# Weight tiles written three ahead of their products, pair sums in pieces and 512 KB loads in a split-precision decoder layer

## The chip, the cores and the metric

The program runs on one core of one Trainium2 chip, as a single launch. The metric is the device time of an execution in microseconds; a kernel's time is the median of its runs. The engines are named as the profile names them: PE (matrix products), PEld (its weight loads), DVE (vector), ACT (scalar), POOL, and SP, which here does nothing but issue DMAs.

## The reference

One decoder layer on 256 tokens of width 4096. All matrices are float32.

```
proj = x @ w_in                          # 4096 x 11280
y_conv = conv_group(c_a, c_b) * silu(c_gate)
y_gla  = gla_group(g_q, g_k, g_v, g_lr) * silu(g_gate)
y_mem  = memory_group(m_q, mem @ w_mem_kv) * silu(m_gate)   # 256 memory tokens, 4096 x 2048
out = concat(y_conv, y_gla, y_mem) @ w_out                  # 4096 x 4096
y = layernorm(ALPHA * x + out, ln_g, ln_b)
```

## The kernel before, in words

Every large product is done in split precision. A weight tile arrives in SBUF as float32 (`raw`); ACT casts it to `hi` (line 89), DVE subtracts `hi` from `raw` to get `lo` (line 90; both in the helper `halves`), and PE does three products for each tile of the activations, which are split in the same way: hi with hi, hi with lo, lo with hi. PE so can't start on a weight tile before ACT has cast it, and can't end it before DVE has made the rest.

The work has four stages in this order.

- **Memory stage** (lines 150 to 192). 32 steps `kt` over the rows of `w_mem`; each step takes 128 rows of 2048 columns, 1024 KB. The first 1024 columns (`mk`) and the last 1024 (`mv`) are two halves of one `raw` tile, split and multiplied apart. After the first step a step's 1024 KB come with one DMA (line 162). Every fourth step a 512 KB unit of the memory tokens (`rawmem`) and one of the tokens x (`rawx`, for the later stages) are loaded and split.
- **Panels** (`panel`, line 277). 23 column panels of `w_in`, each in 8 loads of 1024 KB and 16 weight tiles. The elementwise work of convolution, attention and gates waits in a list, and is taken off it (`do_work`) behind the tiles.
- **Pairs** (`pair`, line 353). Three pairs of 512 output columns of `w_out`, 16 chunks each. A chunk is done either with eight block products or with seven, by Winograd's form of Strassen's method; in the second case DVE makes combinations `tx` and `ty` of the four weight blocks first (lines 398 to 411), and the activations' combinations `eh`, `el` come from `make_sums` (`sums`, line 332, with scratch tiles `r` and `f`). Eight PSUM banks hold a pair's partial products (`N`, `4`, `3`, `2`, `1`, `5`, `6`, `7`). Behind a pair the banks are added into four tiles of the residual `z`, statistics are taken and a row of `ln_g` is multiplied in (lines 1085 to 1115): 20 DVE instructions. The scratch `U` of these sums, `tx` and `f` share one buffer (tag `T`), `ty` and `r` another (tag `S`).
- **Last two panels and the layer norm** (lines 1119 to 1152).

All pools rotate: three `raw` buffers, four `hi` and four `lo`. The text of the kernel does not set the order on an engine: the program is built with `tile.TileContext(nc, schedule_with_timeline_sim=True)` (line 1232), and a scheduler places the instructions of each engine by a timeline of its own, with the text's order as the wish. On the chip each engine then works its list strictly from the top. All loads are issued by SP; eight completion semaphores rotate, and in the built program a load waits until the one eight places ahead of it in SP's list has landed.

Of the kernel before, what the change touches and what calls it, by code (L numbers as in the profile page):

```python
# [9 lines left out]
F32 = mybir.dt.float32  # L10
# [18 lines left out]
EARLY = 5  # L29

# [18 lines left out]
def layer_kernel(ctx, tc, xT, memT, xres, w_mem, w_in, w_pairs, w_last, cst, w_gate,  # L49
# [103 lines left out]
    for kt in range(KT):  # L153
# [123 lines left out]
    def panel(chunks, width, stat, fills=0, apart=0, soon=KT // 2):  # L277
# [3 lines left out]
        for tt in range(2):  # L281
            serial[0] += 1
            banks.append(acc.tile([P, 512], F32, tag="acc", name=f"acc_{serial[0]}"))
        held = []
# [14 lines left out]
        for c in range(KT // 2):  # L299
            if c % 2 == 0:  # L300
                raw = w_raw([P, 4, width], "w")
                nc.sync.dma_start(out=raw, in_=chunks[c // 2].rearrange("p (k n) -> p k n", k=4))
            hi, lo = w_tiles([P, 2, width], "w", KT // 2 - apart <= c < KT // 2 - WBUFS)
            halves(raw[:, 2 * (c % 2) : 2 * (c % 2) + 2, :], hi, lo)
            if c >= KT // 2 - apart:
                held.append((c, hi, lo))
            else:
                for w in (hi, lo):
                    for tt in range(2):
                        mms(c, tt, w, w is lo)  # L310
            left = max(1, soon - c)
            do_work(-(-len(work) // left))
            for _ in range(min(fills, len(fill))):
                fill.popleft()()
        if not apart:
            return banks

        def rest(k, tt):
            c, hi, lo = held[k]
            for w in (hi, lo):  # L320
                mms(c, tt, w, w is lo)

        return banks, rest
# [29 lines left out]
    def pair(chunks, order, stat, ext, soon=KT // 2):  # L353
# [3 lines left out]
        for pool, tag, names in ((acc, "acc", "N432"), (sm, "sm", "1567")):  # L357
            for nm in names:
                serial[0] += 1
                banks[nm] = pool.tile([P, 512], F32, tag=tag, name=f"{tag}_{nm}_{serial[0]}")  # L360

# [28 lines left out]
        for n, (c, by7, tiles) in enumerate(plan):  # L390
            raw = w_raw([P, 4, 512], "w")
            nc.sync.dma_start(out=raw, in_=chunks[c].rearrange("p (k n) -> p k n", k=4))
            w = {}
            if by7:
                serial[0] += 1
                x = tmp.tile([P, 2, 512], F32, tag="T", name=f"tx_{serial[0]}", bufs=1)
                y = tmp.tile([P, 2, 512], F32, tag="S", name=f"ty_{serial[0]}", bufs=1)
                nc.vector.tensor_tensor(
                    out=x,
                    in0=raw[:, 3:4, :].to_broadcast([P, 2, 512]),  # L400
                    in1=raw[:, 0:3:2, :],
                    op=ALU.subtract,
                )
                nc.vector.tensor_tensor(
                    out=y[:, 0, :], in0=raw[:, 2, :], in1=x[:, 0, :], op=ALU.subtract
                )
                nc.vector.tensor_tensor(
                    out=y[:, 1, :], in0=raw[:, 1, :], in1=y[:, 0, :], op=ALU.subtract
                )
                src = dict(a=raw[:, 0:2, :], c=raw[:, 2:3, :], x=x, y=y)  # L410
            else:
                src = dict(a=raw[:, 0:2, :], b=raw[:, 2:4, :])
            for nm, terms in tiles:
                m = 1 if nm == "c" else 2
                w[nm] = tuple(t[:, :m, :] for t in w_tiles([P, 2, 512], "w"))
                halves(src[nm], *w[nm])
                for second in range(2):
                    for j, (slot, st, bk) in enumerate(terms):
                        sh, sl = st(c)
                        for s in (sh,) if second else (sh, sl):  # L420
                            nc.tensor.matmul(  # L421
                                banks[bk],
                                lhsT=s,
                                rhs=w[nm][second][:, slot, :],
                                start=first[bk] == (n, nm, j) and not second and s is sh,
                                stop=last[bk] == (n, nm, j) and second == 1,
                            )
            do_work(-(-len(work) // max(1, soon - n)))
        return banks
# [405 lines left out]
    off = 0  # L835
    for name, i, ranges in PANELS:
        width = sum(n for _, n in ranges)
        size = 16 * P * 2 * width
        chunks = w_in[off : off + size].rearrange("(c p f) -> c p f", c=8, p=P)
        off += size  # L840
        banks = panel(chunks, width, lambda u: x_units[u], fills=2)
# [87 lines left out]
    for hi, lo in x_units:  # L929
        give(hi, lo)  # L930
    assert not fill
# [144 lines left out]
    for u in (4, 5):  # L1076
        work.append(lambda u=u: make_sums(u))
    for j in range(3):
        if j == 1:
            work.append(lambda: make_sums(6))  # L1080
        n0, n1 = 2 * j, 2 * j + 1
        load_res(n0)
        load_res(n1)
        b = pair(w_pairs[j], orders[j], stat, lambda u: extT[u], soon=KT // 2 if j else 8)
        rows = [spread(ln_g, n0, "Ah"), spread(ln_g, n1, "Al")]

        def add(y, ps, first=False):
            if first:
                nc.vector.scalar_tensor_tensor(
                    out=y, in0=y, scalar=ALPHA, in1=ps, op0=ALU.mult, op1=ALU.add  # L1090
                )
            else:
                nc.vector.tensor_tensor(out=y, in0=y, in1=ps, op=ALU.add)  # L1093

        z11, z21 = z[n0][:, 0, :], z[n0][:, 1, :]
        z12, z22 = z[n1][:, 0, :], z[n1][:, 1, :]
        add(z22, b["N"], True)
        add(z12, b["3"], True)
        add(z11, b["2"], True)
        add(z21, b["4"], True)  # L1100
        serial[0] += 1
        t = tmp.tile([P, 2, 512], F32, tag="T", name=f"U_{serial[0]}", bufs=1)
        u2, u3 = t[:, 0, :], t[:, 1, :]
        nc.scalar.copy(out=u2, in_=b["1"])
        add(z11, b["1"])
        nc.vector.tensor_tensor(out=u2, in0=u2, in1=b["6"], op=ALU.add)
        add(z12, b["5"])
        add(z22, b["5"])
        nc.vector.tensor_tensor(out=u3, in0=u2, in1=b["7"], op=ALU.add)
        add(z12, u2)  # L1110
        add(z21, u3)
        add(z22, u3)
        for n, tt, y in ((n0, 0, z11), (n1, 0, z12), (n0, 1, z21), (n1, 1, z22)):
            nc.vector.bn_stats(out=stats[:, tt, n, :], in_=y)
            nc.vector.tensor_tensor(out=y, in0=y, in1=rows[n - n0], op=ALU.mult)  # L1115
    for e in extT.values():
        give(*e)
# [126 lines left out]
```

## Time and profile before

| | us |
|---|---|
| median of 3 runs (1563.94 to 1565.36) | 1564.78 |
| the profiled execution | 1562.82 |
| its span, first to last instruction | 1561.1 |
| PE busy | 1523.4 |
| DVE busy | 1069.3 |
| ACT busy | 769.7 |

The span is what the trace shows; the profiled execution's own time has 1.7 us more that lie around it. Busy times of different engines overlap and don't add up.

### The profile page before, as it was taken

What the parts mean: (1) busy time and instruction counts of PE and PEld (TensorE: products, weight loads), DVE (VectorE), ACT (ScalarE), POOL (GpSimd) and SP (SyncE); (2) the same over time, 40 slices, a digit from 0 to 9 for tenths busy, and PEclk for the clock granted to TensorE, in tenths of its full rate; (3) what the DMA queues carried; (4) which work ended last, traced back from release to release, by engine and by line L of the source; (5) the groups of instructions that cost most, each with busy time, mean ns of one, the idle gap of its engine ahead of it and who ended that gap; (6) DMA issues with size and microseconds to landing.
All of it is one profiled execution on the core that took longest, in us unless ns stands there. A gap on an engine that the chain in (4) does not pass through costs nothing.

```text
span 1561.1 us, 18190 instructions
## 1 busy us (share of the span) xinstructions
PE 1523.4 (98%) x6929; PEld 1288.4 (83%) x6929; DVE 1069.3 (68%) x1361; ACT 769.7 (49%) x936; POOL 46.8 (3%) x59
## 2 busy tenths in 40 slices
PE   7999999999999999999999999999999998989997
PEld 5888888888888888999998888888888876878885
DVE  6554564999999555757574555556576697887965
ACT  6443454444465444664454554455555434545541
POOL 0000000000000000003030000000000000000001
PEclk9999999999999999999999999999999998999998
DMA  9665555555555655455545555555567545546562
GB/s 358 245 216 191 192 199 199 180 199 189 189 172 180 216 189 189 158 191 174 173 158 198 189 191 212 189 191 195 199 225 269 189 162 196 195 175 217 206 219 108
DMA packets 49184, 307.52 MB, mean 197 GB/s; under 512 B 5508, under 2 KB 6404, under 8 KB 18504
## 3 DMA queue, kind: packets, MB, share of 16 engines
q1 hardware_dynamic: 49096, 306.36, 55.8%
q8 instruction: 54, 0.88, 0.2%
q14 instruction: 34, 0.28, 0.0%
HBM read 302.14 MB, written 4.19 MB: 196 GB/s over the span
## 4 chain that ended last, share of the span: by engine, by line
PE 94%; DVE 3%; DMA 2%; issue 0%; ACT 0%; SPq 0%; POOL 0%; DVEq 0%; ACTq 0%
PE acc L291 67%; PE acc L421 9%; PE mk L181 5%; PE mv L181 5%; PE sm L421 3%; PE acc_N L421 3%; DMA rawwm<-w_mem 1%; DMA rawx<-xT 1%; DVE low L90 1%; PE o L272 1%; PE A L682 1%; DVE xr L1093 0%; PE sc L272 0%; PE mo L272 0%; DVE xr L1115 0%
## 5 line engine op out<-in xcount | busy, mean ns | idle before, releaser
L90 DVE TENSOR_TENSOR low<-raww,hiw 128x1024 fp32r<-128x1024 f32 (+3 forms) x496 | 586.3, 1187 | 329.5 <-ACT hiw L89 316.2
L89 ACT CAST hiw<-raww 128x1024 fp32r<-128x1024 f32 (+3 forms) x496 | 499.4, 1012 | 556.3 <-PE acc L291 470.6
L291 PE MATMUL acc<-hiw,hx 128*128 128x512 f32 (+2 forms) x1472 | 560.3, 381 | 0.0
L291 PE MATMUL acc<-hiw,lx 128*128 128x512 f32 (+2 forms) x1472 | 560.3, 381 | 0.0
L291 PE MATMUL acc<-low,hx 128*128 128x512 f32 (+2 forms) x1472 | 381.6, 380 | 0.0
L291 PEld LDWEIGHTS acc<-hiw,hx 128*128 128x128 f32 x1472 | 276.3, 188 | 45.4
L291 PEld LDWEIGHTS acc<-hiw,lx 128*128 128x128 f32 x1472 | 276.3, 188 | 45.2
L291 PEld LDWEIGHTS acc<-low,hx 128*128 128x128 f32 x1472 | 275.2, 188 | 45.5
L90 DVE TENSOR_TENSOR lowm<-rawwm,hiwm 128x1024 fp32r<-128x1024 f32 (+2 forms) x68 | 78.5, 1161 | 77.7 <-ACT hiwm L89 75.7
L89 ACT CAST hiwm<-rawwm 128x1024 fp32r<-128x1024 f32 (+2 forms) x68 | 67.7, 1003 | 89.4 <-PE mk L181 41.3
L421 PE MATMUL acc<-hiw,xh 128*128 128x512 f32 x224 | 88.0, 393 | 16.2 <-ACT hiw L89 16.2
L770 DVE SCALAR_TENSOR_TENSOR cacc<-hT,cst_sb,cacc 128x231 f32<-128x231 f32 (+29 forms) x240 | 97.9, 461 | 0.1
L421 PE MATMUL acc<-hiw,xl 128*128 128x512 f32 x224 | 87.6, 391 | 0.0
L421 PE MATMUL acc<-low,xh 128*128 128x512 f32 x224 | 66.9, 390 | 0.0
L421 PEld LDWEIGHTS acc<-hiw,xh 128*128 128x128 f32 x224 | 42.2, 189 | 25.8 <-ACT hiw L89 17.1
L181 PE MATMUL mk<-hiwm,hmem 128*128 128x512 f32 (+1 forms) x132 | 52.3, 398 | 9.3 <-ACT hiwm L89 9.3
L181 PE MATMUL mk<-hiwm,lmem 128*128 128x512 f32 (+1 forms) x132 | 51.8, 394 | 0.0
L239 ACT COPY S<-T 32x256 f32<-32x256 f32 x112 | 45.2, 404 | 9.9 <-DVE T L224 8.5
L181 PE MATMUL mv<-hiwm,hmem 128*128 128x512 f32 x128 | 50.0, 391 | 0.0
L291 PE MATMUL acc<-hiw,xh 128*128 128x512 f32 x128 | 49.9, 390 | 0.0
L181 PE MATMUL mv<-hiwm,lmem 128*128 128x512 f32 x128 | 49.8, 389 | 0.0
L291 PE MATMUL acc<-hiw,xl 128*128 128x512 f32 x128 | 49.8, 389 | 0.0
(231 smaller groups left out, 1327.9 us busy)
## 6 DMA issues: line engine op xcount, KB each, us to landing
raww<-w_in SPq DMA_DIRECT2D x144, 1024.0 KB
raww<-w_pairs SPq DMA_DIRECT2D x48, 1024.0 KB
rawwm<-w_mem SPq DMA_DIRECT2D x31, 1024.0 KB
raww<-w_in SPq DMA_DIRECT2D x32, 824.0 KB
raww<-w_last SPq DMA_DIRECT2D x16, 1024.0 KB
raww<-w_in SPq DMA_DIRECT2D x8, 832.0 KB
rawx<-xT SPq DMA_DIRECT2D x8, 512.0 KB
xr<-xres SPq DMA_DIRECT2D x8, 512.0 KB
```

Of the source, the lines that this page charges most:

```text
L89: nc.scalar.copy(out=hi, in_=src)
L90: nc.vector.tensor_tensor(out=lo, in0=src, in1=hi.bitcast(F32), op=ALU.subtract)
L181: nc.tensor.matmul(mem_banks[half * 4 + a // 512 * 2 + mt][:, a % 512 : a % 512 + step], lhsT=s[:, kt % 4, mt * P : (mt + 1) * P], rhs=w[: ...
L239: f(out=to[32 * b : 32 * b + 32, :, :, a, :], in_=frm[32 * a : 32 * a + 32, :, :, b, :],)
L272: nc.tensor.matmul(ps, lhsT=a, rhs=b, start=t == 0 and k == 0, stop=t == n - 1 and k == 2)
L291: nc.tensor.matmul(banks[tt][:, :width], lhsT=s[:, kt % 4, tt * P : (tt + 1) * P], rhs=w[:, k, :], start=kt == 0 and not second and s is s ...
L421: nc.tensor.matmul(banks[bk], lhsT=s, rhs=w[nm][second][:, slot, :], start=first[bk] == (n, nm, j) and not second and s is sh, stop=last[b ...
L682: nc.tensor.matmul(ps[:, at : at + n], lhsT=keys[:, j, k0 : k0 + P], rhs=qs[:, j, q0 : q0 + n], start=dk == 0, stop=dk == 1,)
L770: nc.vector.scalar_tensor_tensor(out=a, in0=h, scalar=dw_sb[:, cb, j : j + 1], in1=a, op0=ALU.mult, op1=ALU.add)
```

## The change

The halves of a memory step are loaded by a DMA of 512 KB each. Weight tiles pass through a queue, `stream`: `push` writes a tile's load and its split, and the products of a tile are written when three more tiles have been pushed (`AHEAD = 3`). What stands behind a pair or a panel (evacuations, sums, further loads) is hung on the last tile's products with `after`. A pair's sums fall into a first part (`close`) and pieces in a second queue, `later`, one of which is written behind each tile that follows. The pieces need one scratch tile `u2` in place of two, and 20 DVE instructions as before, in another order. PSUM banks of a pair are taken when first used.

```diff
         raw = w_raw([P, 2, 1024], "wm")
-        if kt:
-            nc.sync.dma_start(out=raw, in_=w_mem[kt].rearrange("p (h n) -> p h n", h=2))
         for half in range(2):
+            if kt:
+                nc.sync.dma_start(
+                    out=raw[:, half, :], in_=w_mem[kt][:, 1024 * half : 1024 * half + 1024]
+                )
             wt = (raw[:, half, :], *w_tiles([P, 1024], "wm"))
...
+    stream = deque()
+    later = deque()
+
+    def push(make, use):
+        make()
+        stream.append(use)
+        while len(stream) > AHEAD:
+            stream.popleft()()
+
+    def after(f):
+        if stream:
+            g = stream.pop()
+            stream.append(lambda: (g(), f()))
+        else:
+            f()
...
+        for c in range(KT // 2):
+            push(lambda c=c: make(c), lambda c=c: use(c))
+        after(lambda: then(banks))
...
+        for n, (_, _, tiles) in enumerate(plan):
+            for i in range(len(tiles)):
+                push(lambda n=n, i=i: make(n, i), lambda n=n, i=i: use(n, i))
+        after(lambda: then(banks))
...
+    def close(n0, b):
+        z11, z21 = z[n0][:, 0, :], z[n0][:, 1, :]
+        z12, z22 = z[n0 + 1][:, 0, :], z[n0 + 1][:, 1, :]
+        add(z22, b["N"], True)
+        add(z12, b["3"], True)
+        add(z21, b["4"], True)
+        add(z11, b["2"], True)
+        rows = [spread(ln_g, n0, "Ah"), spread(ln_g, n0 + 1, "Al")]
...
+        def one():
+            nc.scalar.copy(out=u2, in_=b["1"])
+            add(z11, b["1"])
+
+        def two():
+            add(u2, b["6"])
+            add(z12, b["5"])
+
+        def three():
+            add(z22, b["5"])
+            add(z12, u2)
+
+        def four():
+            add(u2, b["7"])
+            add(z21, u2)
+
+        def five():
+            add(z22, u2)
+
+        def stat_scale(n, tt):
+            y = z[n][:, tt, :]
+            nc.vector.bn_stats(out=stats[:, tt, n, :], in_=y)
+            nc.vector.tensor_tensor(out=y, in0=y, in1=rows[n - n0], op=ALU.mult)
+
+        later.extend((one, two, three, four, five))
+        for n in (n0, n0 + 1):
+            for tt in range(2):
+                later.append(lambda n=n, tt=tt: stat_scale(n, tt))
...
     for j in range(3):
         if j == 1:
-            work.append(lambda: make_sums(6))
...
+            after(lambda: work.append(lambda: make_sums(6)))
+        after(lambda j=j: (load_res(2 * j), load_res(2 * j + 1)))
+        pair(
+            w_pairs[j],
+            orders[j],
+            stat,
+            lambda u: extT[u],
+            lambda b, j=j: close(2 * j, b),
+            soon=KT // 2 if j else 8,
+        )
```

In the lists that the scheduler makes of it, three places differ from before. The first is SP's list in the memory stage. `rawwm` is a tile of `w_mem`, `rawx` and `rawmem` are the 512 KB units; the last row here, `rawwm_296`, is step kt 4. Before:

```order
L116 DMA rawx_284<-xT 128x1024
L162 DMA rawwm_236<-w_mem 128x2048
L116 DMA rawmem_290<-memT 128x1024
L116 DMA rawx_432<-xT 128x1024
L116 DMA rawmem_438<-memT 128x1024
L116 DMA rawx_580<-xT 128x1024
L116 DMA rawmem_586<-memT 128x1024
L116 DMA rawx_728<-xT 128x1024
L116 DMA rawmem_734<-memT 128x1024
L116 DMA rawx_876<-xT 128x1024
L116 DMA rawmem_882<-memT 128x1024
L162 DMA rawwm_296<-w_mem 128x2048
```

The same place now; `rawwm_299` is kt 4, `rawwm_334` is kt 5:

```order
L117 DMA rawx_287<-xT 128x1024
L117 DMA rawmem_293<-memT 128x1024
L117 DMA rawx_439<-xT 128x1024
L117 DMA rawmem_445<-memT 128x1024
L117 DMA rawx_591<-xT 128x1024
L117 DMA rawmem_597<-memT 128x1024
L117 DMA rawx_743<-xT 128x1024
L164 DMA rawwm_299<-w_mem 128x1024 x2
L117 DMA rawmem_749<-memT 128x1024
L117 DMA rawx_895<-xT 128x1024
L117 DMA rawmem_901<-memT 128x1024
L164 DMA rawwm_334<-w_mem 128x1024 x2
```

The two halves of kt 4 now stand ahead of the last three units and no longer behind them; kt 5 follows those three. Step kt 3 (`rawwm_236` before) now stands ahead of the first `rawx`, so that the same loads as before lie ahead of the unit `rawx_743`.

The second place is DVE's list between pair 0 and pair 1. `xr` are the residual tiles that take pair 0's sums, `r`, `f` and `el` belong to `make_sums(6)`, `tx` and `ty` to the first seven-product chunk of pair 1. Before (`r` is made 23 rows further up, among pair 0's last sums, and the first two `f` two rows further up):

```order
L1115 TENSOR_TENSOR xr_8889<-xr_8889,row_9531 128x512
L1115 TENSOR_TENSOR xr_8891<-xr_8891,row_9533 128x512
L347 TENSOR_TENSOR f_9604<-f_9604,r_9603 128x2x128
L347 TENSOR_TENSOR f_9604<-r_9603,f_9604 128x2x128
L90 TENSOR_TENSOR el_9611<-f_9604,eh_9610 128x1024
L398 TENSOR_TENSOR tx_9650<-raww_9648 128x1024
L404 TENSOR_TENSOR ty_9651<-raww_9648,tx_9650 128x512
L407 TENSOR_TENSOR ty_9651<-raww_9648,ty_9651 128x512
```

Now:

```order
L439 TENSOR_TENSOR tx_9613<-raww_9611 128x1024
L1181 BN_STATS zstats<-xr_8938 128x6
L1182 TENSOR_TENSOR xr_8936<-xr_8936,row_9582 128x512
L445 TENSOR_TENSOR ty_9614<-raww_9611,tx_9613 128x512
L1182 TENSOR_TENSOR xr_8938<-xr_8938,row_9584 128x512
L448 TENSOR_TENSOR ty_9614<-raww_9611,ty_9614 128x512
L91 TENSOR_TENSOR low_9668<-ty_9614,hiw_9667 128x1024
L91 TENSOR_TENSOR low_9686<-tx_9613,hiw_9685 128x1024
L371 TENSOR_TENSOR r_9638<-xh_8786,xl_8787 128x1024
L91 TENSOR_TENSOR low_9696<-raww_9693,hiw_9695 128x1024
```

`make_sums(6)` went from ahead of `tx` and `ty` to behind their low halves; its later rows follow one by one between further `low` rows. All sums of the pair still stand ahead of the second `ty`.

The third place is ACT's list at the same boundary, where `eh` is the cast of `make_sums(6)`. Before:

```order
L89 CAST hiw_9662<-raww_9648 128x1024
L89 CAST eh_9610<-f_9604 128x1024
L89 CAST hiw_9672<-ty_9651 128x1024
L89 CAST hiw_9682<-tx_9650 128x1024
L89 CAST hiw_9694<-raww_9692 128x1024
```

Now:

```order
L90 CAST hiw_9649<-raww_9611 128x1024
L90 CAST hiw_9667<-ty_9614 128x1024
L90 CAST hiw_9685<-tx_9613 128x1024
L90 CAST hiw_9695<-raww_9693 128x1024
L90 CAST hiw_9708<-raww_9693 128x1024
L90 CAST hiw_9723<-raww_9721 128x1024
L90 CAST hiw_9737<-raww_9721 128x1024
L90 CAST hiw_9762<-raww_9755 128x512
L90 CAST hiw_9778<-raww_9755 128x1024
L90 CAST eh_9645<-f_9639 128x1024
```

`eh` moved nine casts down. In the panels PE's and ACT's lists are the same as before but for some rows about the attention over the memory tokens.

## Rows read from the trace of the kernel before

**Rows 1.** The page, part 1: busy time, share of the span, instructions.

```profile
PE 1523.4 (98%) x6929; PEld 1288.4 (83%) x6929; DVE 1069.3 (68%) x1361; ACT 769.7 (49%) x936; POOL 46.8 (3%) x59
```

**Rows 2.** Waits of PE: who, for whom, us in total, times, longest.

```profile
PE acc L421 <- ACT hiw L89: 16.2, 2, 10.8
PE mk L181 <- ACT hiwm L89: 9.3, 3, 7.6
```

**Rows 3.** Timeline of PE, memory stage: start, us, operation, idle before and releaser.

```profile
12.86 0.50 PE L181 MATMUL mk<-hiwm,hmem 128*128 128x512 f32 x1 [1.58 <-ACT hiwm L89]
...
28.41 1.07 PE L181 MATMUL mv<-lowm,hmem 128*128 128x512 f32 x4
37.07 0.80 PE L181 MATMUL mk<-hiwm,hmem 128*128 128x512 f32 x1 [7.59 <-ACT hiwm L89]
...
44.47 0.39 PE L181 MATMUL mk<-hiwm,hmem 128*128 128x512 f32 x1
```

**Rows 4.** Timeline of ACT, memory stage.

```profile
3.10 0.40 ACT L89 CAST hmem<-rawmem 128x256 fp32r<-128x256 f32 x1 [1.01 <-DMA rawmem<-memT]
...
25.75 1.05 ACT L89 CAST hmem<-rawmem 128x1024 fp32r<-128x1024 f32 x1 [1.36 <-DMA rawmem<-memT]
...
33.41 1.04 ACT L89 CAST hmem<-rawmem 128x1024 fp32r<-128x1024 f32 x1 [0.23 <-DMA rawmem<-memT]
35.97 1.99 ACT L89 CAST hiwm<-rawwm 128x1024 fp32r<-128x1024 f32 x2 [1.51 <-DMA rawwm<-w_mem]
```

**Rows 5.** The chain that ended last: start, us, what.

```profile
44.64 2.72 PE mk L181 x12
```

**Rows 6.** Windows: us, busy PE, PEld, DVE, ACT, POOL; PEclk, DMA share, GB/s.

```profile
38.00:39.00 1.00, 1.00 (x4) 0.71 (x3) 1.00 (x2) 0.53 (x1) 0.00 (x0) 0.50 1.01 410
460.00:480.00 20.00, 20.00 (x101) 17.01 (x100) 19.87 (x35) 12.55 (x21) 0.00 (x0) 1.00 0.50 163
1300.00:1320.00 20.00, 20.00 (x88) 16.47 (x88) 15.55 (x17) 8.63 (x9) 0.00 (x0) 0.99 0.55 200
```

**Rows 7.** Timeline of PE at the two boundaries between pairs.

```profile
1294.83 0.79 PE L421 MATMUL acc<-hiw,xh 128*128 128x512 f32 x1 [10.81 <-ACT hiw L89]
...
1300.52 0.39 PE L421 MATMUL acc_N<-hiw,xl 128*128 128x512 f32 x1
...
1386.14 0.79 PE L421 MATMUL acc<-hiw,xh 128*128 128x512 f32 x1 [5.40 <-ACT hiw L89]
...
1389.27 0.39 PE L421 MATMUL sm<-hiw,el 128*128 128x512 f32 x1
```

**Rows 8.** Timeline of ACT between pair 0 and pair 1.

```profile
1288.63 1.04 ACT L89 CAST eh<-f 128x1024 fp32r<-128x1024 f32 x1 [11.90 <-DVE f L347]
1293.73 1.04 ACT L89 CAST hiw<-ty 128x1024 fp32r<-128x1024 f32 x1 [4.06 <-DVE ty L407]
```

**Rows 9.** Timeline of DVE between pair 0 and pair 1.

```profile
1268.87 1.22 DVE L337 TENSOR_TENSOR r<-xh,xl 128x1024 f32<-128x1024 f32 x1
1270.00 1.22 DVE L90 TENSOR_TENSOR low<-raww,hiw 128x1024 fp32r<-128x1024 f32 x1
...
1285.26 0.74 DVE L347 TENSOR_TENSOR f<-r 128x256 f32<-128x256 f32 x2
1285.92 1.89 DVE L1115 TENSOR_TENSOR xr<-xr,row 128x512 f32<-128x512 f32 x3
1287.72 0.42 DVE L347 TENSOR_TENSOR f<-f,r 128x256 f32<-128x256 f32 x1
...
1289.71 1.23 DVE L90 TENSOR_TENSOR el<-f,eh 128x1024 fp32r<-128x1024 f32 x1 [1.11 <-ACT eh L89]
1290.97 1.22 DVE L398 TENSOR_TENSOR tx<-raww 128x1024 f32<-128x1024 f32 x1
...
1292.95 0.69 DVE L407 TENSOR_TENSOR ty<-raww,ty 128x512 f32<-128x512 f32 x1
```

**Rows 10.** Timeline of SP: the first load's issue.

```profile
0.81 0.39 SPq L116 DMA_DIRECT2D rawmem<-memT  x1
```

More of the change, by code (lines that the diff above doesn't have):

```diff
@@ L274, in products, with flush, panel @@
                 )
-    def panel(chunks, width, stat, fills=0, apart=0, soon=KT // 2):
+    stream = deque()
[11 more added lines that the diff above has]
+            f()
+    def flush():
+        while stream:
+            stream.popleft()()
+    def panel(chunks, width, stat, then, fills=0, apart=0, soon=KT // 2):
         banks = []
[L281 to L284, printed above, removed]
+        held = {}
+        raw = {}
         def mms(c, tt, w, second):
@@ L388, in pair @@
                     last[bk] = (n, nm, j)
[L390 to L428, printed above, removed]
@@ new lines, in use @@
+        def use(n, i):
+            c, by7, tiles = plan[n]
+            nm, terms = tiles[i]
+            w = st.pop((n, nm))
+            for second in range(2):
+                for j, (slot, stationary, bk) in enumerate(terms):
+                    sh, sl = stationary(c)
+                    for s in (sh,) if second else (sh, sl):
+                        nc.tensor.matmul(
+                            bank_of(bk),
+                            lhsT=s,
+                            rhs=w[second][:, slot, :],
+                            start=first[bk] == (n, nm, j) and not second and s is sh,
+                            stop=last[bk] == (n, nm, j) and second == 1,
+                        )
+            if later:
+                later.popleft()()
+            if i == len(tiles) - 1:
+                do_work(-(-len(work) // max(1, soon - n)))
@@ L834, in layer_kernel, with projected @@
     sig = {}
[L835 to L841, printed above, removed]
+    def projected(name, i, width, banks):
         if name in ("mq", "q", "k"):
@@ L928, in layer_kernel, with give_x @@
             work.append(mixm)
-    for hi, lo in x_units:
-        give(hi, lo)
-    assert not fill
+    off = 0
+    for name, i, ranges in PANELS:
+        width = sum(n for _, n in ranges)
+        size = 16 * P * 2 * width
+        chunks = w_in[off : off + size].rearrange("(c p f) -> c p f", c=8, p=P)
+        off += size
+        panel(
+            chunks,
+            width,
+            lambda u: x_units[u],
+            lambda banks, name=name, i=i, width=width: projected(name, i, width, banks),
+            fills=2,
+        )
+    def give_x():
+        for hi, lo in x_units:
+            give(hi, lo)
+        assert not fill
+    after(give_x)
     keys = [("gla", i) for i in range(4)] + [("conv", i) for i in range(2)] + [
@@ L1078, in layer_kernel, with queue_sums @@
+    def queue_sums():
+        for u in (4, 5):
+            work.append(lambda u=u: make_sums(u))
+    after(queue_sums)
     for j in range(3):
         if j == 1:
-            work.append(lambda: make_sums(6))
[L1081 to L1093, printed above, removed]
@@ L1107, in layer_kernel @@
[L1107 to L1117, printed above, removed]
-    for j in range(4):
-        work.append(lambda j=j: rows_gb(j))
@@ new lines, in give_sums, with close6 @@
+    def give_sums():
+        for e in extT.values():
+            give(*e)
+        for j in range(4):
+            work.append(lambda j=j: rows_gb(j))
+    after(give_sums)
+    after(lambda: (load_res(6), load_res(7)))
+    def close6(banks):
+        g = spread(ln_g, 6, "S")
+        for tt in range(2):
+            residual(tt, 6, banks[tt])
+            y = z[6][:, tt, :]
+            nc.gpsimd.tensor_tensor(out=y, in0=y, in1=g, op=ALU.mult)
+    panel(w_last[0], 512, stat, close6)
+    banks = []
```

113 lines of the change are left out of this document (68 added, 45 removed).

## The prediction

> **What bounds the kernel now.** I began with the page's busy times: PE works 1523.4 us of a span of 1561.1 us [rows 1]. Whatever the change does to ACT, DVE or the loads, it can only win in the 37.7 us in which PE has nothing to do, or where PE runs at half its clock. So the second view is PE's own waits [rows 2]: two waits of 16.2 us together in the pairs, one of them 10.8 us, and three of 9.3 us in the memory stage. Both lines name ACT's cast as the releaser, but a releaser is only the last link, so the third view is the timeline of each engine around the long waits.
>
> In the memory stage the long wait lies before step kt 4. PE's products of kt 3 begin their last piece at 28.41 us, and those of kt 4 start at 37.07 us after 7.59 us of nothing [rows 3]. ACT cast kt 4 at 35.97 us, and itself waited for the load [rows 4]. So DMA bounds this place. The reader is to see the rhythm there: the units of x and the memory tokens land one behind the other; from the cast at 25.75 to that at 33.41 there are six of 512 KB, 1.28 us each, and kt 4, 1024 KB, takes 2.56 us behind the last [rows 4]. The queue is full and serves its loads in their order; kt 4 is late because units are ahead of it that nobody needs yet. After the wait PE runs at a granted clock of 0.50, the 1.2 GHz level [rows 6], and kt 4's products take 37.07 to 44.47, 7.40 us [rows 3]; at 2.4 GHz twelve products take 2.72 us, a step of 24 thus 5.44 [rows 5]. The slow clock costs 1.96 us.
>
> Between pair 0 and pair 1 the wait of PE is 10.81 us [rows 7]. ACT waited 11.90 us for `f` before it could cast `eh`, and only then came to the cast of `ty`, for which it waited again, 4.06 us [rows 8]. DVE meanwhile is the engine that works without a pause: sums, `r`, `f`, `el`, and only then `tx` and `ty` [rows 9]. So DVE's list bounds this place, and ACT's list, which is worked from the top, hangs on it. Behind the wait 13 products take from 1294.83 to 1300.52, 5.69 us, where 13 at full clock take 2.95 (2.72 / 12 each [rows 5]): 2.74 us for the clock. The boundary between pairs 1 and 2 waits 5.40 us without any `make_sums`, and pays for 7 products 3.13 us in place of 1.59, 1.54 us of slow clock [rows 7].
>
> Everywhere else PE is full. In 460 to 480 us, for instance, DVE is busy 19.87 of 20 us, and PE still 20.00 [rows 6].
>
> **The memory stage, part by part.** The order of SP shows the same loads as before up to the unit `rawx_743`, whose counterpart lands before three more units and kt 4. In the old rhythm it lands three units of 1.28 us ahead of 33.41, at 29.57 us (35.97 - 2.56 - 3 x 1.28). Now kt 4's first half follows it: 29.57 + 1.28 = 30.85 us. PE started 1.10 us behind the cast's start before (35.97 to 37.07), so it starts kt 4 at about 31.95. The second half lands at 32.13, ahead of its need. Then the three units take 3.84 us, and the first half of kt 5 lands at 30.85 + 1.28 + 3.84 + 1.28 = 37.25; PE can start kt 5 at 38.35. Its products of kt 4 end at 31.95 + 5.44 = 37.39, so a second, small wait of about 1.0 us appears there: that is what is late next. Before, kt 5 started at 44.47 [rows 3]. **Gain 6.1 us.** If the clock falls again in the wait before kt 4, kt 4 ends at 39.35, and the gain is 5.1 us. I take the first: the shortest wait in this trace behind which the clock is seen at half is 5.40 us [rows 7], and the new wait is about 3.7 us.
>
> The early halves of kt 1 also arrive sooner: half of 1024 KB is 1.28 us, out of a wait of 1.58 [rows 3]. This costs and gains nothing: PE then reaches kt 4 1.3 us earlier and waits so much longer there, for the load sets the start. Products with `lo` of the `mk` half stand before the `mv` half in the first steps now; eight `hi` products take 1.8 us, a cast of 1.05 and a subtraction of 1.23 overlap all but 0.5 us of that [rows 4, 9], once, at a place that waits for the load anyway. Beyond kt 5, kt 6 is complete at about 41, three units and kt 7's first half at 46, and PE needs kt 7 at 38.4 + 2 x 5.44 = 49.2: covered by 2 us; if that cover went, it would be at most a microsecond. The 31 more issues of 0.39 us [rows 10] lie on SP, which waits most of the time for buffers.
>
> One rule speaks against halves. Loads of 512 KB moved one per 1.28 us, loads of 1024 KB one per 2.56 [rows 4], so a half costs half. The Trainium skill, SBUF — State Buffer, section The DMA setup-cost knee, has every transfer pay about 2 us whatever its size. By its fit an estimate of two halves is 6.4 us against 4.4 for the whole, longer than the 5.44 us of a step's products; 31 steps would then lose 30 us. By that rule, in a full queue, the trace does not agree.
>
> **The pair boundaries.** Ahead of `tx` and `ty` DVE loses `r`, 1268.87 to 1270.00, 1.13 us; the first two `f`, 1285.26 to 1285.92, 0.66 us; and the rest of `make_sums(6)` with its wait for `eh`, 1287.72 to 1290.97, 3.25 us [rows 9]. Together 5.04 us. The pair's sums don't leave: all 20 of them still stand ahead of the second `ty`, only in another order. So `ty` ends 5.04 us earlier, ACT's cast of `ty` no longer stands behind `eh`, and PE starts 5.04 us earlier: **gain 5.0 us**, and a wait of about 5.8 us stays, with DVE's sums as its cause. A wait of that length costs 1.54 us of slow clock, as at the next boundary, in place of 2.74 [rows 7]: **gain 1.2 us**, with 0 and 2.7 as its bounds. The moved rows, 3.9 us of DVE without the wait, come behind, where DVE is busy 15.55 of 20 us and PE full [rows 6]; `el` is used by the last seven-product chunks of pair 1 only. If that cover went, they would cost PE up to 3.9 us. At the second boundary the same sums precede the same `ty`: 0.
>
> **The queue of three tiles itself.** In the panels and the chunks the scheduler had already written splits ahead, and the lists show the same order; only rows around the memory attention change places, where PE is full [rows 6]. No instruction is added but the issues. Cost 0, bounds -1 and +1 us.
>
> **Sum.** -6.1 - 5.0 - 1.2 = -12.3 us. The profiled execution, 1562.82, would become 1550.5. The median of the runs shown lies 1.96 us above it, so I say 1564.8 - 12.3 = **1552.5 us**.
>
> **Rivals.** (a) Only the boundary gains: kt 4 or kt 5 stays as late as now, since the 16 DMA engines don't serve the loads as evenly as I read it. For it: a landing is that of its slowest part, which I can't see. Against: the even 1.28 us. 1564.8 - 6.2 = 1558.6. (b) Only the memory stage gains: at the boundary something else ends last, such as PE's own last sums into a bank, or the cast of a tile that waits for a buffer. For it: ACT's casts there wait for PE too. Against: DVE has no pause ahead of `tx`. 1564.8 - 6.1 = 1558.7. (c) The change does not do what it says: the scheduler had hoisted everything, and what moved was hidden: 1564.8, no difference. Against: two moves that stand in the lists. (d) Slower: halves pay their start one after the other. The first load, 128 KB, was issued at 0.81 and its cast began at 3.10 [rows 4, 10], 2.29 us. If each half cost 2.29 + 1.28 us, a step would take 7.14 us against 5.44: 31 x 1.70 = 53 us more, less 6.2 at the boundary, 1611 us. It decides from 2.72 us per half on. Against it stands the rhythm again. The Trainium skill's rule, named above, would act in this way.
>
> **How the numbers follow.** A measurement of this kernel can tell 0.2%, 3.1 us, from no change. Forecast 0.78; (a) 0.08; (b) 0.07; (c) 0.04; (d) 0.03. Faster: the first three, 0.93; same 0.04; slower 0.03. The range takes in the forecast with its bounds (1549.5 if all slow clock at the boundary goes and a little more; 1556 if the clock falls at kt 4, the moved rows cost PE and the panels lose 1) and reaches to (a) and (b) at 1558.7: 1549.5 to 1559.
>
> **What would show it.** Right: PE's wait before kt 4 near 4 us and a small one before kt 5, kt 5's products from about 38.4 us; the waits at both boundaries between 5 and 6 us, and ACT's cast of `eh` without a long wait ahead of the cast of `ty`. Wrong: a wait for loads that comes back after kt 7, waits of PE inside pair 1, or units and halves that land more than 1.5 us apart.

## The result, and the profile after

The changed kernel takes 1550.88 us (median of 4 runs, 1550.24 to 1551.56); the kernel before, run beside it, 1564.36 us. The ratio is 0.9917, 95% interval 0.99 to 0.9934: faster by 0.83%. The profiled execution took 1550.68 us; its span is 1549.0 us, 12.1 us less than the span before.

PE does the same 6929 products, and its busy time is the same to 1.4 us [rows 1]. The page of the changed kernel, part 1:

```profile
PE 1522.0 (98%) x6929; PEld 1286.7 (83%) x6929; DVE 1070.0 (69%) x1361; ACT 770.9 (50%) x936; POOL 46.9 (3%) x59
```

What shrank is its waits. The waits of PE in the changed kernel (who waits for whom, us in total, times, longest), which answer to [rows 2]: 16.2 us became 10.8 in the pairs, 9.3 became 4.3 in the memory stage.

```profile
PE acc L465 <- ACT hiw L90: 10.8, 2, 5.5
PE mk L184 <- ACT hiwm L90: 4.3, 3, 2.4
```

The memory stage on PE's timeline of the changed kernel (start, us, operation, idle before and releaser). These rows are the starts of kt 1, kt 4 and kt 5 [rows 3]:

```profile
12.51 0.50 PE L184 MATMUL mk<-hiwm,hmem 128*128 128x512 f32 x1 [1.22 <-ACT hiwm L90]
...
31.53 0.50 PE L184 MATMUL mk<-hiwm,hmem 128*128 128x512 f32 x1 [2.39 <-ACT hiwm L90]
...
37.94 0.50 PE L184 MATMUL mk<-hiwm,hmem 128*128 128x512 f32 x1 [0.67 <-ACT hiwm L90]
```

kt 5 starts at 37.94 us where it started at 44.47: **6.5 us**. Two things make it: kt 4 starts 5.54 us earlier (31.53 in place of 37.07), and its products run at full clock, which shortens the step from 7.40 to 6.41 us, the 0.67 us wait before kt 5 included. The window that showed 0.50 before [rows 6] now shows, in the column behind the busy times, the 2.4 GHz level:

```profile
38.00:39.00 1.00, 1.00 (x5) 0.82 (x6) 1.00 (x1) 0.88 (x1) 0.00 (x0) 1.00 1.01 401
```

ACT's timeline in the same stage shows why kt 4 came earlier. Its two halves are cast at 30.43 and 31.72 us, where its 1 MB was cast at 35.97 [rows 4]; the units of memory and x that used to stand ahead of it come behind it, and the rhythm of 1.27 to 1.29 us per 512 KB is the same:

```profile
29.08 1.05 ACT L90 CAST hx<-rawx 128x1024 fp32r<-128x1024 f32 x1 [0.22 <-DMA rawx<-xT]
30.43 1.04 ACT L90 CAST hiwm<-rawwm 128x1024 fp32r<-128x1024 f32 x1 [0.30 <-DMA rawwm<-w_mem]
31.72 1.06 ACT L90 CAST hiwm<-rawwm 128x1024 fp32r<-128x1024 f32 x1 [0.24 <-DMA rawwm<-w_mem]
...
36.84 1.05 ACT L90 CAST hiwm<-rawwm 128x1024 fp32r<-128x1024 f32 x1 [0.31 <-DMA rawwm<-w_mem]
```

At the pair boundaries PE's timeline of the changed kernel answers to [rows 7]. In each pair of rows the first is the product behind the wait, the second the one from which products follow each other at full clock again, or nearly:

```profile
1282.90 0.79 PE L465 MATMUL acc<-hiw,xh 128*128 128x512 f32 x1 [5.51 <-ACT hiw L90]
...
1286.36 0.39 PE L465 MATMUL acc<-low,xh 128*128 128x512 f32 x1
...
1373.00 0.80 PE L465 MATMUL acc<-hiw,xh 128*128 128x512 f32 x1 [5.28 <-ACT hiw L90]
...
1378.28 0.44 PE L465 MATMUL acc_N<-hiw,xh 128*128 128x512 f32 x1
```

The first wait fell from 10.81 to 5.51 us, **5.3 us**. Eight slow products behind it took 3.46 us, 1.65 us more than eight at full clock (2.72 / 12 each [rows 5]); before, the slow clock cost 2.74 there. At the second boundary the wait hardly moved (5.40 to 5.28), but twelve products are slow now, 5.28 us, 2.56 us of slow clock against 1.54. So the clock gave 1.09 us at one boundary and took 1.02 at the other. The sum of all places: 6.53 + 5.30 + 1.09 + 0.12 - 1.02 = 12.0 us of the 12.1.

ACT's timeline at the first boundary shows the turn of order. Before, the cast of `eh` came first, and that of `ty` behind it [rows 8]. Now `ty` comes first, and `eh` ten us later without any wait:

```profile
1281.80 1.05 ACT L90 CAST hiw<-ty 128x1024 fp32r<-128x1024 f32 x1 [10.79 <-DVE ty L448]
...
1292.29 1.05 ACT L90 CAST eh<-f 128x1024 fp32r<-128x1024 f32 x1
```

And DVE's timeline there [rows 9]. The first row is the last pair of sums that read `U`; `tx` starts 2.4 us after its start, and `r`, the first row of `make_sums(6)`, stands behind `ty`:

```profile
1275.11 1.28 DVE L1147 TENSOR_TENSOR xr<-xr,U 128x512 f32<-128x512 f32 x2
...
1277.51 1.21 DVE L439 TENSOR_TENSOR tx<-raww 128x1024 f32<-128x1024 f32 x1
...
1281.03 0.68 DVE L448 TENSOR_TENSOR ty<-raww,ty 128x512 f32<-128x512 f32 x1
...
1285.16 1.22 DVE L371 TENSOR_TENSOR r<-xh,xl 128x1024 f32<-128x1024 f32 x1
```

### The profile page after: what moved, and what is told of

Its sections match the earlier page's. It is cut to its first block, busy times and chain, and to the rows that moved or that the text cites. A ratio compares the mean times of both kernels' runs of the same rounds, so it can differ in the third digit from the quotient of the medians.

```text
span 1549.0 us, 18217 instructions
## 1 busy us (share of the span) xinstructions
PE 1522.0 (98%) x6929; PEld 1286.7 (83%) x6929; DVE 1070.0 (69%) x1361; ACT 770.9 (50%) x936; POOL 46.9 (3%) x59
## 4 chain that ended last, share of the span: by engine, by line
PE 94%; DVE 2%; DMA 2%; issue 0%; SPq 0%; ACT 0%; POOL 0%; DVEq 0%; ACTq 0%
PE acc L315 67%; PE acc L465 10%; PE mk L184 5%; PE mv L184 5%; PE sm L465 3%; PE acc_N L465 3%; DMA rawwm<-w_mem 1%; DMA rawx<-xT 1%; PE o L275 1%; PE A L733 1%; DVE low L91 0%; DVE xr L1147 0%; PE sc L275 0%; PE mo L275 0%; DVE zstats L1181 0%
## 5 line engine op out<-in xcount | busy, mean ns | idle before, releaser
L465 PE MATMUL acc<-hiw,xh 128*128 128x512 f32 x224 | 87.6, 393 | 10.8 <-ACT hiw L90 10.8
```

The costliest lines, as they stand in the source:

```text
L465: nc.tensor.matmul(bank_of(bk), lhsT=s, rhs=w[second][:, slot, :], start=first[bk] == (n, nm, j) and not second and s is sh, stop=last[bk] ...
```

## The experiments

The prediction's own account was two gains that have nothing to do with each other, one made by which loads stand ahead of kt 4, the other by where `make_sums(6)` stands. Its rivals gave the gain to the queue of tiles, to the pieces, or to the size of the loads as such. Each run has theories of its own, lettered anew. The first five runs take the change apart. The next six ask what the waits that are left hang on. Ratios are to the kernel before on the same chip, where it took 1561.97 to 1562.66 us; the times below are to be read against that, some 2 us under the 1564.36 above. A difference of medians to the change's 1550.88 so makes a run look up to 2 us better than it is; the ratios, the spans, and `pieces_off`, which ran beside `hold`, `hold_1mb` and `u_own`, are the safer comparison.

| run | median us | ratio, 95% interval | span | PE's wait before kt 4, kt 5 | at boundary 0 to 1 | 1 to 2 |
|---|---|---|---|---|---|---|
| the change | 1550.88 | 0.9917, 0.99 to 0.9934 | 1549.0 | 2.39, 0.67 | 5.51 | 5.28 |
| halves_only | 1556.32 | 0.9959, 0.9947 to 0.9971 | 1554.6 | 1.77, none | 10.81 | 5.40 |
| no_halves | 1557.29 | 0.9963, 0.9951 to 0.9976 | 1557.6 | 6.46, none | 5.50 | 5.28 |
| sums6_late | 1558.95 | 0.9973, 0.9962 to 0.9984 | 1556.0 | 5.82, none | 5.63 | 5.40 |
| ahead0 | 1556.46 | 0.9956, 0.9945 to 0.9968 | 1554.3 | 2.33, 0.66 | 10.69 | 5.28 |
| pieces_off | 1550.53 | 0.9923, 0.991 to 0.9935 | 1550.8 | 2.09, 0.67 | 5.63 | 5.40 |
| hold | 1547.57 | 0.9901, 0.9888 to 0.9915 | 1545.7 | none | 5.50 | 5.28 |
| hold_1mb | 1547.64 | 0.9903, 0.9888 to 0.9918 | 1545.8 | none | 5.50 | 5.28 |
| u_own | 1538.61 | 0.9844, 0.9831 to 0.9858 | 1536.2 | 1.96, 0.62 | 0.90 | 0.56 |
| u_early | 1544.94 | 0.9889, 0.9875 to 0.9902 | 1542.8 | 1.85, 0.65 | 5.60, one tile group later | 0.55 |
| both | 1535.43 | 0.9825, 0.9812 to 0.9838 | 1534.4 | none | 0.90 | 0.56 |
| before_both | 1535.40 | 0.983, 0.9816 to 0.9843 | 1533.7 | none | 0.90 | 0.55 |

### The halves alone, on the kernel before

```
-            nc.sync.dma_start(out=raw, in_=w_mem[kt].rearrange("p (h n) -> p h n", h=2))
         for half in range(2):
+            if kt:
+                nc.sync.dma_start(
+                    out=raw[:, half, :], in_=w_mem[kt][:, 1024 * half : 1024 * half + 1024]
+                )
```

> The kernel before, with one edit: each 1 MB weight load of the memory stage is made as two of 512 KB. Theory A (two independent gains; the memory stage alone carries its 6.5 us): kt 5 starts at 37.9 as in the change, the wait at the first pair boundary stays 10.8 us, the time is 6.5 us below the kernel before, 1557.0 to 1559.0 us (the slow clock behind the boundary waits may move it by 1 us). Theory B (the gain needs the queue of tiles): kt 5 starts at 44.5 and the time is that of the kernel before. Theory C (a half pays a start of its own): the CASTs of the memory stage come every 3 us or so and the time is above that of the kernel before.

Measured 1556.32 us, 6.3 us under the kernel before (0.9959): theory A on the amount, and just below the range that I had put in absolute times, since the kernel before took 1562.66 here. The waits of PE in this run: the pairs' line is that of the kernel before to the digit, only the memory stage's is smaller.

```profile
PE acc L423 <- ACT hiw L89: 16.2, 2, 10.8
...
PE mk L183 <- ACT hiwm L89: 3.7, 3, 1.8
```

Theory C, a start paid per half, is out: the casts of kt 4's two halves come 1.28 us apart here too.

One thing went otherwise than in the changed kernel. kt 4 started even earlier, at 30.89 us behind a wait of 1.77 us, and yet kt 5 did not start before 38.08 us, because the clock fell in the middle of kt 4:

```profile
30.89 0.50 PE L183 MATMUL mk<-hiwm,hmem 128*128 128x512 f32 x1 [1.77 <-ACT hiwm L89]
...
33.21 1.91 PE L183 MATMUL mk<-lowm,hmem 128*128 128x512 f32 x4
...
38.08 0.39 PE L183 MATMUL mk<-hiwm,hmem 128*128 128x512 f32 x1
```

The granted clock from 33 to 35 us is 0.50; four products take 1.91 us there and 1.07 at full clock [rows 3]. The step lasts 7.19 us where its products need 5.44 [rows 5], and that is why no wait is left ahead of kt 5.

### The change without the halves

```
+            if kt:
+                nc.sync.dma_start(out=raw, in_=w_mem[kt].rearrange("p (h n) -> p h n", h=2))
         for half in range(2):
-            if kt:
-                nc.sync.dma_start(
...
```

> The changed kernel with the 1 MB loads of the memory stage put back. Theory A: kt 5 starts at 44.5 again, the first boundary wait stays at 5.5 us, the time is 6.5 us above the changed kernel, about 1557 us (1556.5 to 1558.5). Theory B (the halves are worth nothing, the queue brought it all): 1551 us, kt 5 at 38.

Measured 1557.29 us, 0.9963 where the change has 0.9917: about 7 us worse (0.0046 x 1562.66), with an uncertainty of some 3 us. The long wait before kt 4 is back and the boundary's stays short: theory A. In the profiled execution 1.4 us of the difference is slow clock at the boundaries, 2.68 + 2.90 us here against 1.65 + 2.56. The waits of PE:

```profile
PE acc L463 <- ACT hiw L90: 11.1, 3, 5.5
PE mk L182 <- ACT hiwm L90: 7.9, 3, 6.5
```

### Nothing but a later make_sums(6)

```
         if j == 1:
+            pause(3)
             work.append(lambda: make_sums(6))
```

> The kernel before, with one edit: the sums of unit 6 are queued three chunks later, no queue of tiles, no pieces, 1 MB loads. Theory A (the boundary gain is the five DVE rows and one CAST of make_sums(6) that no longer stand ahead of the tx and ty of the next products): the first boundary wait falls from 10.8 to about 5.5 us, the second stays at 5.4, the time is 5.0 to 6.3 us below the kernel before, 1558 to 1559.5 us. Theory B (the pieces or the queue of three tiles did it): the wait stays near 10.8 us and the time within 1 us of the kernel before.

This is the kernel before with one line more. Measured 1558.95 us, 0.9973: 3.7 us under the kernel before by the medians (2.5 to 5.9 by the interval) where 5.0 to 6.3 were expected. The waits of PE in this run:

```profile
PE acc L421 <- ACT hiw L89: 11.0, 2, 5.6
PE mk L181 <- ACT hiwm L89: 7.3, 3, 5.8
```

The first boundary's wait is 5.63 us, nearly as in the changed kernel, without its queue or its pieces: theory A on the mechanism. In the profiled execution part of the gain went to the clock, and kt 5 starts 0.61 us earlier than before (43.86 for 44.47), a place that the edit, in the pairs, does not touch. Ten products are slow behind the first boundary and fourteen behind the second, together 5.02 us of slow clock, where the kernel before paid 2.74 + 1.54 = 4.28.

### The change with a queue of no tiles

```
-AHEAD = 3
+AHEAD = 0
```

> The changed kernel with a queue of no tiles (each tile's products are written right behind it), pieces and halves kept. In its order make_sums(6) stands ahead of tx and ty again. Theory A (the queue is worth something only because it carries make_sums(6) three tiles further): the first boundary wait is back at about 10.8 us, the rest as in the changed kernel, the time 5 to 6 us above it, 1556 to 1557 us. Theory B (the prediction's own term: tiles made ahead are worth nothing): 1551 us. Theory C (making tiles ahead hides waits elsewhere too): waits appear in the panels and the time is above 1558 us.

Measured 1556.46 us, 0.9956 where the change has 0.9917: about 6 us worse, theory A. DVE's timeline at the first boundary of this run has the rows in the order of the kernel before [rows 9], `r`, `f` and `el` ahead of `tx`:

```profile
1262.61 1.22 DVE L371 TENSOR_TENSOR r<-xh,xl 128x1024 f32<-128x1024 f32 x1
...
1283.33 1.23 DVE L91 TENSOR_TENSOR el<-f,eh 128x1024 fp32r<-128x1024 f32 x1 [1.11 <-ACT eh L90]
1284.59 1.23 DVE L439 TENSOR_TENSOR tx<-raww 128x1024 f32<-128x1024 f32 x1
```

So the queue of three tiles is what moves `make_sums(6)` in the changed kernel: `do_work` runs when a tile is used, which is three tiles after it is made. Elsewhere the queue is worth nothing: no wait of PE in the panels or chunks came or went. The prediction's term of 0 for the queue so holds for the panels and chunks only; for the whole kernel, as theory B reads it, it fails.

### The change with a pair's sums all at once

```
-        later.extend((one, two, three, four, five))
+        for f in (one, two, three, four, five):
+            f()
...
-                later.append(lambda n=n, tt=tt: stat_scale(n, tt))
+                stat_scale(n, tt)
```

> The changed kernel with a pair's end sums written all at once again, behind the pair's last tile, as before; queue and halves kept. Theory A (the pieces are worth nothing: the row that frees the shared buffer for tx is the last sum, wherever the others stand): boundary waits 5.5 to 5.9 us each, time within 1 us of the changed kernel. Theory B (the pieces make the boundary gain): a wait of 8 us or more, time 3 us or more above the changed kernel.

Measured 1550.53 us, 0.9923 against 0.9917; boundary waits 5.63 and 5.40 us, 0.12 us more each than with the pieces. The second wait lies a tenth under the 5.5 to 5.9 us that were expected. Theory A: the pieces are worth nothing that a run can tell.

### Holding the other loads back

```
-                nc.sync.dma_start(
+                wd = nc.sync.dma_start(
                     out=raw[:, half, :], in_=w_mem[kt][:, 1024 * half : 1024 * half + 1024]
...
-            x_units.append(load_unit("x", four(xT[kt // 4])))
+            with tc.issue_after(wd.ins):
+                x_units.append(load_unit("x", four(xT[kt // 4])))
```

The memory units' line gets the same two words around it. `issue_after` only fixes the place in SP's list: the load stands behind the weight load `wd`.

> The changed kernel with the loads of x and of the memory's later units queued behind the weight loads of their own step, so that they no longer stand ahead of the weights of kt 4. Theory A (what is left of the memory stage's wait is the order of the loads): no wait over 0.5 us before kt 4 and kt 5, kt 5 starts at about 35 us (37.9 less 2.39 and 0.67), the time is 3 us below the changed kernel. Theory B (the rate of the loads is the bound): the wait only moves to a later step, and the time is within 1 us of the changed kernel.

Measured 1547.57 us, 0.9901. That is 3.3 us below the changed kernel by the medians and by the spans, but only 2.5 by the ratios, whose intervals overlap. Against `pieces_off`, which ran beside it, it is 3.0 us, and the slowest execution here (1547.93) is under the fastest there (1550.21). On PE's timeline both waits are gone, and kt 5 starts at 34.59 us in place of 37.94: theory A. Windows of this run, in the stretch of the wait (us, busy PE, PEld, DVE, ACT, POOL; PEclk, DMA share, GB/s):

```profile
28.00:38.00 10.00, 10.00 (x46) 8.27 (x45) 6.13 (x6) 5.51 (x6) 0.00 (x0) 1.00 0.83 300
```

The same window of the kernel before:

```profile
28.00:38.00 10.00, 2.40 (x9) 1.73 (x8) 8.37 (x8) 7.31 (x8) 0.00 (x0) 0.81 1.02 419
```

PE does 46 products there where it did 9, and the DMA engines are no longer full. The kernel before moved 419 GB/s there, but about half of it was units that PE needs later: four of 512 KB landed between 29 and 34 us, by their casts [rows 4].

> As the run with the loads held back, but with the 1 MB weight loads of the kernel before. Theory A (the 7.6 us wait was made by what stood ahead of the weights, the size only decided how much of it was felt): no wait over 1 us before kt 4 and kt 5 either, time within 1.5 us of the run with held loads and halves. Theory B (the size itself is worth 6.5 us): a wait of 5 us or more before kt 4, time 5 us or more above the run with halves.

This run has the same edit and the 1 MB loads. Measured 1547.64 us, 0.07 us from the run with halves. **Of the two sizes neither is worth anything over the other once the order is right**: theory A, and what the halves did in the change was to let kt 4 slip in three units further ahead. The waits of PE in the memory stage:

```profile
PE mk L183 <- ACT hiwm L90: 1.8, 2, 1.7
...
PE mv L183 <- ACT hiwm L90: 0.6, 1, 0.6
```

Both lie before 14 us, where the first loads come; there is none at kt 4 or behind it. The Trainium skill, DMA: Bandwidth & Descriptors, section Measured (HBM→SBUF, 128 partitions, SWDGE, issued from GpSimd), advises batches of 1 MiB or more. These two runs show no price for 512 KB, but in them the products and no longer the loads set the pace (DMA share 0.83 above), so they could hide a small one. That a full queue charges none shows in the changed kernel: 1.27 to 1.29 us for 512 KB, where the kernel before took 2.56 for 1 MB.

### A buffer of its own for U

```
-        u2 = tmp.tile([P, 512], F32, tag="T", name=f"U_{serial[0]}", bufs=1)
+        u2 = tmp.tile([P, 512], F32, tag="U", name=f"U_{serial[0]}", bufs=1)
...
-            after(lambda: work.append(lambda: make_sums(6)))
+            after(lambda: (pause(4), work.append(lambda: make_sums(6))))
```

> The changed kernel with a buffer of its own for U (the end sums' scratch, until now in the same buffer as tx), and make_sums(6), which uses that buffer as well, four chunks later. Theory A (the 5.4 us left at each boundary are tx waiting for the last use of U): both boundary waits fall below 1.5 us, the slow products behind them go too, the time is 11 to 14 us below the changed kernel, 1537 to 1540 us. Theory B (tx and ty wait for DVE's own queue of sums, or for their load): the waits stay over 4 us and the time within 3 us of the changed kernel.

`U` and `tx` have the same tag and one buffer, so `tx` has to wait for the last sum that reads `U`. Measured 1538.61 us, 0.9844: theory A. What put the sums ahead of `tx` at both boundaries, and with them the 5.4 us, was neither the amount of DVE's work nor a load, but a shared buffer: DVE does the same sums here, busy 1068.7 us against 1070.0, only no longer all ahead of `tx` and `ty`. The waits of PE in the pairs:

```profile
PE acc L465 <- ACT hiw L90: 2.2, 3, 0.9
```

DVE's timeline of this run at the first boundary: `tx` now starts before the sums on `U`, and `ty` ends amid them.

```profile
1264.60 1.22 DVE L439 TENSOR_TENSOR tx<-raww 128x1024 f32<-128x1024 f32 x1
...
1267.47 0.68 DVE L1147 TENSOR_TENSOR U<-U,sm 128x512 f32<-128x512 f32 x1
...
1274.54 0.68 DVE L448 TENSOR_TENSOR ty<-raww,ty 128x512 f32<-128x512 f32 x1
...
1278.07 1.28 DVE L1147 TENSOR_TENSOR xr<-xr,U 128x512 f32<-128x512 f32 x2
```

The span is 12.8 us below that of the changed kernel. Of this, 4.61 + 4.72 are the two waits less the 0.90 and 0.56 us that stay; 0.73 comes back at the next group of tiles (the third wait of that line); and 1.65 + 2.56 us of slow clock are gone, for behind these short waits only the first product is slower, by 0.1 us each. That makes 12.5.

The second line of the edit was tested by leaving it out.

> The changed kernel with U in a buffer of its own, and make_sums(6) left where the change has it. Theory A (make_sums(6) uses the buffers of tx and ty, so wherever it stands the next tx waits for its CAST): the boundary waits fall under 1.5 us, but a wait of 5 to 6 us comes back some 10 us later, at the next tile that needs tx, and the time lies 5 to 8 us above the run with make_sums(6) four chunks later, 1544 to 1546.5 us. Theory B (the shared buffer of U was all): as that run, 1538.6 us.

Measured 1544.94 us, 0.9889: 6.3 us worse than with it by the medians, 7.0 by the ratios, theory A. `make_sums(6)` writes `r` and `f` into the buffers of `ty` and `tx`, so the wait moves with it. ACT's timeline of this run, one group of tiles later, shows the pattern of the kernel before [rows 8] again:

```profile
1292.46 1.05 ACT L90 CAST eh<-f 128x1024 fp32r<-128x1024 f32 x1 [6.16 <-DVE f L381]
1297.58 1.04 ACT L90 CAST hiw<-ty 128x1024 fp32r<-128x1024 f32 x1 [4.08 <-DVE ty L448]
```

### Both repairs, on either kernel

The two edits above together, first on the changed kernel.

> The changed kernel with both repairs: the loads of x and memory held behind their step's weights, and U in a buffer of its own with make_sums(6) four chunks later. Theory A (the two are independent): the gains of the two runs add, 3.3 and 12.3 us below the changed kernel, 1534.5 to 1536.5 us; on PE no wait over 1 us between 15 us and the last stage. Theory B (they share DMA or DVE time): less than 13 us together.

Measured 1535.43 us, 0.9825: 15.4 us below the changed kernel by the medians, 3.3 + 12.3 = 15.6 by the single runs; by the ratios 0.0092 where the single runs give 0.0016 + 0.0073 = 0.0089. The gains add, and the longest wait of PE between 15 us and the last stage is 0.90 us: theory A.

Then on the kernel before, with nothing of the change:

```
-            work.append(lambda: make_sums(6))
+            pause(5)
+            work.append(lambda: make_sums(6))
...
-        t = tmp.tile([P, 2, 512], F32, tag="T", name=f"U_{serial[0]}", bufs=1)
-        u2, u3 = t[:, 0, :], t[:, 1, :]
+        t = tmp.tile([P, 512], F32, tag="U", name=f"U_{serial[0]}", bufs=1)
+        u2 = u3 = t
...
-        nc.vector.tensor_tensor(out=u3, in0=u2, in1=b["7"], op=ALU.add)
         add(z12, u2)
+        nc.vector.tensor_tensor(out=u3, in0=u2, in1=b["7"], op=ALU.add)
...
-            nc.sync.dma_start(out=raw, in_=w_mem[kt].rearrange("p (h n) -> p h n", h=2))
+            wd = nc.sync.dma_start(out=raw, in_=w_mem[kt].rearrange("p (h n) -> p h n", h=2))
...
+            with tc.issue_after(wd.ins):
```

> The kernel before with the same two repairs and nothing of the change: no queue of tiles, no pieces, 1 MB loads; U in a buffer of its own (2 KB a partition, with its second half written in place) and make_sums(6) five chunks later, the loads of x and memory held back. Theory A (queue, pieces and 512 KB loads carry nothing of their own): within 2 us of the run with both repairs on the changed kernel, 1535 to 1538 us. Theory B (the queue is needed for tx and ty to go ahead of the sums): a wait of 4 us or more at each boundary, 1545 us or more.

Measured 1535.40 us, 0.03 us from the run on the changed kernel: theory A. The waits of PE of this run in the pairs and in the memory stage:

```profile
PE acc L423 <- ACT hiw L89: 2.2, 3, 0.9
PE mk L182 <- ACT hiwm L89: 1.8, 2, 1.5
```

So a dozen lines on the kernel before give 27 us where the whole change gives 13, and with these lines in place the queue, the pieces and the 512 KB loads add nothing. By the ratios that is 1.7% under the kernel before and 0.9% under the changed kernel.

## Why the prediction was right, point by point

The forecast was 1552.5 us in a range of 1549.5 to 1559; measured 1550.88.

- **The memory stage, -6.1 us: right.** Measured -6.5 (kt 5 at 37.94 in place of 38.35). The step to kt 4 was right to 0.4 us (31.53 for 31.95). The wait itself was put at about 3.7 us and was 2.39: kt 1's wait shrank by 0.36 us only, not by 1.3, so PE came to kt 4 later than the prediction had it. That half of the step cancelled, as the prediction said it would, because the load sets the start. The small new wait before kt 5 was 0.67 for about 1.0. One of the stated signs of being wrong did appear: two units were cast 1.88 us apart (23.35 and 25.23 us), where 1.5 was the limit. It was one gap; the loads behind it kept the rhythm up to kt 6.
- **No fall of the clock before kt 4: right, by luck.** The granted clock is 1.00 behind the wait of 2.39 us. But the reason given, that 5.40 us was the shortest wait in the trace with the clock at half behind it, misread the trace. In the last stage of the kernel before, PE waited 4.27 us for DVE, and the granted clock was 0.50 behind that:

```profile
1551.45 0.47 PE L1016 MATMUL ccT<-ident,cc 128*128 128x128 f32 x1 [4.27 <-DVE cc L994]
...
1553.00:1555.00 2.00, 2.00 (x6) 1.10 (x4) 1.89 (x3) 0.00 (x0) 0.00 (x0) 0.50 0.81 303
```

And in the run with the halves alone the clock fell behind 1.77 us, the shortest wait before kt 4 of all the runs that have one. The length of the wait does not settle it. In six profiles with the halves and nothing held back the clock stayed up five times.

- **The halves' own price, 0: right.** The rhythm stayed at 1.28 us per 512 KB, and with the right order of loads halves and wholes are 0.07 us apart. Steps without a wait take the 5.44 us of their products: with the loads held back, ACT's casts of weights come 2.72 us apart on the mean (nine casts from 31.16 to 52.92 us), two to a step of products. So rival (d) is out. The Trainium skill's SBUF — State Buffer, section The DMA setup-cost knee, would have a step's two halves take 6.4 us, by the estimate in the prediction; no run here shows such a price.
- **make_sums(6), -5.0 us: right.** Measured -5.30, and shown alone with one line on the kernel before: 5.63 us of wait is left there, without anything else of the change. The 3.9 us of moved rows cost PE nothing, as said.
- **The wait that stays, about 5.8 us: right in size (5.51), wrong in its cause.** The prediction held that DVE's sums make it, all 20 of them ahead of the second `ty`. They do stand there, but not because DVE has no time: it does the same sums in the run with a buffer for `U`, and the wait is 0.90 us. `tx` stood behind them because it is written into `U`'s buffer. The size came out because those rows are what PE waits through, whatever put them there.
- **The slow clock, -1.2 us: mis-sized.** At the first boundary it was -1.09, near the forecast. But the prediction priced it by the length of the wait and put the second boundary at 0. There it was +1.02 with no longer a wait. Together the clock gave 0.07 us. The bounds of 0 to 2.7 held this. Whether the change moved the second boundary's clock, or one execution differs there from the next, one profile of each kernel can't tell.
- **The queue of three tiles, 0 in the panels and chunks: right.** What it does, it does through `make_sums(6)`: without it the first wait is 10.69 us again. The pieces are worth nothing either.
- **Rivals (a), (b) and (c)** each kept one of the two gains, or none. Both came: kt 5 moved by 6.5 us and the first boundary by 6.4 with its clock.

Sum: -12.3 forecast, -12.1 in the profiled execution; the medians differ by 13.5, within the interval of the ratio (10.3 to 15.6 us). That the sum is met to 0.2 us is luck: the two waits gave 0.8 us more than forecast (with 0.12 at the second boundary), the clock 1.1 less.

## What to carry to other kernels

When a wait ends with a load in a full queue, first read what stands ahead of it and whether anybody needs that yet; here the right order was worth all that the smaller loads gave and 3 us more, and with it their size made no difference. When an engine's list seems to be the bound, ask which buffer the late row writes and who read it last: here one shared tag cost 9 us of waits and some 4 us of slow clock, and every row that writes the same buffer, such as `make_sums(6)`, brings the wait along. And take a change apart before building on it: here one line did what looked like the work of a queue and pieces.

## What the runs showed that I had not expected

The price of slow clock behind a wait is not a function of the wait. In the nine runs with a wait of 5.28 to 10.81 us at a boundary (the two kernels and seven of the others), 7 to 14 products behind it run at the 1.2 GHz level: 1.45 to 2.90 us. The extremes are both behind waits of 5.28 us, and the 10.81 us wait cost 2.74 in one run and 1.88 in another. Before kt 4 it is as loose: 1.00 behind 2.39 us in the changed kernel, 0.50 behind 1.77 us in the run with the halves alone. So a boundary wait of five us costs 5 us plus 1.4 to 2.9 here. Executions of one kernel differ in this way too: 30 of the kernel before, taken beside these runs, took 1560.90 to 1566.74 us; those with a mean granted clock of 0.986 took 1564.02 us or more, those with 0.989 or 0.990 at most 1563.21. A difference of a microsecond of slow clock between two single profiles is therefore not shown to come from an edit.

Equal lists of loads did not land equally. Over the six profiles with the halves and nothing held back, kt 4 started anywhere from 30.89 to 33.06 us. Some of it shows as one longer gap between two landings: in the changed kernel ACT waited 0.83 us for a unit at 25.23 us, while in the run with halves alone the casts there stayed 1.25 to 1.29 us apart. The DMA engines of the changed kernel were busy all the while (a share of 1.04 from 24 to 26 us); what they moved in that gap is not shown.
